# Gate products of two branches in both attention halves and the memory steps, memory gates in five tasks

## The chip, the cores and the metric

The kernel runs on one core of a Trainium2 chip. The number that counts is the device time of one execution in microseconds (us). Five engines with their own instruction streams work on it: PE (matrix products), DVE (vector work), ACT (activations such as exp and sigmoid, and copies), POOL (elementwise work) and SP, which here only issues transfers. Each engine takes its instructions strictly in the order in which they stand in its stream, so an instruction that waits holds up all that stand behind it.

## The reference, cut to what matters

Two layers of a trunk over 256 latent tokens and 256 context tokens, 1024 wide. Each layer is a half feed-forward block, a block of three parallel token mixers, and another half feed-forward block; the change lies in the mixer block alone.

```python
def token_mixers(h, hc, need_ctx, ...):             # h: latent, hc: context, normalised
    qa, ka, va, qb, kb, vb, qm, km, vm, om, gm, gl = split_columns(h @ w_in)
    ...
    y_a = windowed_attention(...)                    # branch 0: 8 heads, window 128, sink logit
    y_b = dense_attention(...)                       # branch 1: 8 heads, all keys
    y_m, y_m_c = mlstm_mixer(...)                    # branch 2: conv + silu, scans, 4 heads ("memory")
    y = merge(y_a, y_b, y_m, gl, w_branch, w_out)

def merge(y_a, y_b, y_m, gate_logits, w_branch, w_out):
    y = jnp.stack([y_a, y_b, y_m], axis=-2)
    z = jnp.einsum('btnw,nwd->btnd', y, w_branch)
    g = jax.nn.sigmoid(gate_logits.reshape(gate_logits.shape[:-1] + (N_BRANCH, D_MODEL)))
    return jnp.sum(g * z, axis=-2) @ w_out
```

`gl` are the gate logits: 3 x 1024 columns of the input product, so per branch eight column blocks of 128. They need only the mixer block's input, which is there from the start, not the branches' results. In layer 1 the context tokens need no output any more (`need_ctx` is false), so all of that runs on 256 tokens in place of 512.

## The kernel before, in words

All products are made in fp32 out of rounded pieces: a weight tile is fetched on SP's queue into one of four buffers called raw, ACT writes its rounded part `hi` (L163), DVE the rest `lo` (L164), and each product is then three matmuls, hi·hi, hi·lo and lo·hi (`mm3`, L194 to L196). `run_tasks` goes through one list of tasks, fetches and converts the weights of the next tasks ahead of their use, and calls each task, which writes its instructions; a tile framework then settles the order on each engine, mostly the order of the calls.

`mixer_tasks` builds the list for one mixer block; `weave(a, b)` spreads list b evenly between the members of a. Its stages, in order, and the names used below:

- The input products (q, k, v and so on). W is the number of tokens that need an output, 512 in layer 0 and 256 in layer 1.
- **Attention**, `attn_steps`: one step per branch, block of 128 queries and pair of heads, 16 steps per branch in layer 0 and 8 in layer 1. The steps of branch 0 are the first half, those of branch 1 the second. A step's call writes the scores of its own pair (PE L1012, L1015), their maximum (DVE L1016), the exponentials (ACT L1030), the reciprocal of the sum (DVE L1039) and the normalisation (POOL L1042); then the transposes of the pair scored two steps earlier (PE L1054) with their hi/lo split (ACT L189, DVE L190); then the product with the values of the pair three steps earlier (PE L1069, L1071). So PE, ACT, DVE and POOL form a chain from one step to the next, which is hidden only if PE has other products to make between.
- In the first half these others are `side`: the preparation of the memory's gates (`mgate_steps`: `logsig`, `rows`, `cols`), products of the memory's values (`vm`), the columns of q of branch 1 (`qcols`), and the gate products of branch 0 that are made ahead (`pre_[0]`: 8 in layer 0, 4 in layer 1). In the second half they are the eight convolution tasks (`conv`: 24 matmuls each, then five taps on ACT L956 and DVE).
- **Memory**: `mlstm_steps`: scores (PE L1212), exponentials of the decays (ACT L1225), their products on DVE (L1229), and a step later the sums (PE L1243). With them are woven the merges of branch 0 (`mrg[0]`) and the gate products of branch 1 that are made ahead (`pre_[1]`: 4 in both layers).
- **Merges and readout**: the output gate `om` with `mlstm_readout` (a chain of small DVE operations that ends in L1279), woven with the first half of branch 1's merges; then three more merges; `put_y2`, which transposes the readout (PE L982); the rest of branch 1; branch 2; and the closing.

A gate product is `gate`, 24 matmuls over W columns. `ahead(j)` makes one early: ACT copies it out (L1311), and two of them go as one pair to DRAM (on ACT's queue, L1313). A merge `mk(j)` makes 12 matmuls of branch weights with the branch's result and multiplies by the sigmoid of the gate. For a stored gate the pair is fetched back through SP's queue and one sigmoid is taken of the whole pair, in place (L1328). Otherwise the gate product is made inside the merge and its sigmoid is L1341. Sigmoid, exp and silu belong to different tables of ACT, and a change from one to the other shows in the trace as an ACT_TABLE_LOAD.

`rows` of the memory's gates puts them on 8 partitions as rows (RW), makes four scans and a fifth (L1142, L1144) and ten further DVE operations (L1146 to L1153) into a second buffer (KR), all in one task.

## Time and profile before

| what | before |
|---|---|
| median of 3 runs | 2273.58 us (2269.32 to 2273.76) |
| the profiled execution | 2271.84 us, span 2270.1 us |
| PE busy | 2195.6 us |
| DVE, ACT, POOL busy | 1545.9, 984.6, 133.0 us |
| layer 0: first attention half, second, memory | 129.90, 95.70, 72.10 us |
| layer 1: first attention half, second, memory | 64.60, 66.60, 52.80 us |

The span runs from the first to the last instruction; 1.7 us of the profiled execution's own time lie around it. The stages of the last two rows are cut where PE goes from one to the next. In the rows further below a stage is one line of five engines; what PE's busy time leaves of its length is time in which PE waited. PEclk is the clock granted to PE, 1.00 being the higher of two levels (2.4 GHz), 0.50 the lower (1.2 GHz).

### The profile page before, as it was taken

To read this page: it belongs to the slowest core of one execution; us is meant where nothing else is said; L and a number is where in the kernel's file an instruction comes from. 1 tells how busy PE (TensorE), PEld (TensorE's weight loads), DVE (VectorE), ACT (ScalarE), POOL (GpSimd) and SP (SyncE) were. 2 spreads that over 40 slices of the span, in tenths; PEclk is the share of its full clock that TensorE was granted. 3 is DMA by queue.
4 is the path that set the end of the run, shared out by engine and by line. 5 is a ranking of instruction groups with operands and counts; after the bars stand their busy time and mean duration, and the time that the engine had idled before them with its cause. 6 is when DMAs were issued, how large, how long until landed. Compare 5 with 4: busy or idle time off the path is not lost.

```text
span 2270.1 us, 30607 instructions
## 1 busy us (share of the span) xinstructions
PE 2195.6 (97%) x11666; PEld 1837.6 (81%) x11666; DVE 1545.9 (68%) x2756; ACT 984.6 (43%) x1569; POOL 133.0 (6%) x100
## 2 busy tenths in 40 slices
PE   6999999998999999999999999999999989998998
PEld 4877777787777888888878788777778878997997
DVE  3987775877678664654444378778849787786556
ACT  3322223554588533542222253222226488655444
POOL 0000000013241000000000000000000142000000
PEclk9999999999999999999999999999999999998999
DMA  7665564422213333434433336665634123565554
GB/s 282 214 196 186 165 199 149 125 81 76 94 38 82 119 119 136 142 115 135 129 114 127 103 107 204 195 195 178 223 116 159 57 89 96 167 228 172 189 186 153
DMA packets 126402, 331.36 MB, mean 146 GB/s; under 512 B 12712, under 2 KB 26088, under 8 KB 125488
## 3 DMA queue, kind: packets, MB, share of 16 engines
q1 hardware_dynamic: 111664, 314.02, 43.0%
q10 hardware_dynamic: 14592, 15.40, 2.2%
q8 instruction: 91, 1.49, 0.3%
q14 instruction: 55, 0.45, 0.1%
HBM read 320.91 MB, written 8.47 MB: 145 GB/s over the span
## 4 chain that ended last, share of the span: by engine, by line
PE 84%; DVE 8%; ACT 3%; DMA 2%; issue 2%; POOL 0%; ACTq 0%; POOLq 0%; SPq 0%; DVEq 0%
PE ps L194 26%; PE ps L195 26%; PE ps L196 26%; PE ps L1243 1%; DVE lo L164 1%; DVE sm L1016 1%; ACT t L1030 1%; PE ps L1212 1%; ACT hi L163 1%; PE ps L366 1%; PE ps L1054 1%; PE ps L468 1%; DVE t L190 0%; DVE slot L959 0%; DMA raw<-in_w_gu_dram 0%
## 5 line engine op out<-in xcount | busy, mean ns | idle before, releaser
L163 ACT ACTIVATE hi<-raw 128x1024 fp32r<-128x1024 f32 (+1 forms) x444 | 457.0, 1032 | 766.8 <-PE ps L195 274.7
L194 PE MATMUL ps<-slot,hi 128*128 128x512 f32 (+1 forms) x2232 | 780.5, 351 | 7.7 <-ACT slot L189 5.3
L195 PE MATMUL ps<-slot,hi 128*128 128x512 f32 (+1 forms) x2232 | 776.9, 349 | 0.9 <-DVE slot L190 0.7
L196 PE MATMUL ps<-slot,lo 128*128 128x512 f32 (+1 forms) x2232 | 776.6, 348 | 0.0
L164 DVE TENSOR_TENSOR lo<-raw,hi 128x1024 fp32r<-128x1024 f32 (+1 forms) x444 | 527.1, 1190 | 245.2 <-ACT hi L163 240.7
L194 PEld LDWEIGHTS ps<-slot,hi 128*128 128x128 f32 x2232 | 421.2, 190 | 77.5 <-ACT slot L189 6.6
L195 PEld LDWEIGHTS ps<-slot,hi 128*128 128x128 f32 x2232 | 422.5, 189 | 57.4 <-DVE slot L190 1.7
L196 PEld LDWEIGHTS ps<-slot,lo 128*128 128x128 f32 x2232 | 421.9, 189 | 57.9
L194 PE MATMUL ps<-hi,slot 128*128 128x512 f32 (+2 forms) x1048 | 400.6, 382 | 1.8 <-ACT slot L189 1.1
L196 PE MATMUL ps<-hi,slot 128*128 128x512 f32 (+2 forms) x1048 | 399.5, 382 | 0.0
L195 PE MATMUL ps<-lo,slot 128*128 128x512 f32 (+2 forms) x1048 | 399.5, 381 | 0.0
L358 DVE SCALAR_TENSOR_TENSOR t<-raw,sc,t 128x1024 f32<-128x1024 f32 x224 | 280.5, 1281 | 128.8 <-DMA raw<-in_w_ada_dram 128.5
L1042 POOL TENSOR_SCALAR t<-t,sm 128x512 f32<-128x512 f32 (+1 forms) x96 | 132.9, 1396 | 1767.1 <-DVE sm L1039 1675.7
L194 PEld LDWEIGHTS ps<-hi,slot 128*128 128x128 f32 x1048 | 197.5, 188 | 46.2 <-issue 5.7
L196 PEld LDWEIGHTS ps<-hi,slot 128*128 128x128 f32 x1048 | 197.0, 188 | 39.3
L195 PEld LDWEIGHTS ps<-lo,slot 128*128 128x128 f32 x1048 | 197.3, 188 | 38.8 <-issue 0.2
L189 ACT ACTIVATE slot<-t 128x512 fp32r<-128x512 f32 (+1 forms) x138 | 80.7, 594 | 185.4 <-DVE t L606 160.2
L606 DVE TENSOR_TENSOR t<-ps,t 128x512 f32<-128x512 f32 (+1 forms) x88 | 54.7, 622 | 89.1 <-PE ps L196 87.8
L190 DVE TENSOR_TENSOR slot<-t,slot 128x512 fp32r<-128x512 f32 (+1 forms) x138 | 87.6, 644 | 4.4 <-ACT slot L189 4.1
L1016 DVE TENSOR_REDUCE sm<-ps 128x1 f32<-128x512 f32 (+1 forms) x96 | 54.4, 593 | 22.2 <-PE ps L1015 21.5
L1054 PE MATMUL ps<-ident,t 128*128 128x128 f32 x320 | 47.7, 282 | 18.6 <-POOL t L1042 8.4
L1054 PEld LDWEIGHTS ps<-ident,t 128*128 128x128 f32 x320 | 37.5, 143 | 28.5 <-POOL t L1042 17.3
(198 smaller groups left out, 1670.6 us busy)
## 6 DMA issues: line engine op xcount, KB each, us to landing
raw<-in_w_gu_dram SPq DMA_DIRECT2D x176, 512.0 KB
raw<-in_w_ada_dram SPq DMA_DIRECT2D x128, 512.0 KB
raw<-in_w_down_dram SPq DMA_DIRECT2D x92, 512.0 KB
raw<-in_w_fm_dram SPq DMA_DIRECT2D x64, 512.0 KB
raw<-in_w_br_dram SPq DMA_DIRECT2D x24, 512.0 KB
raw<-in_w_out_dram SPq DMA_DIRECT2D x24, 512.0 KB
...
```

Source lines behind the costliest of these rows:

```text
L163: self.nc.scalar.activation(out=hi, in_=raw, func=AF.Copy)
L164: self.nc.vector.tensor_tensor(out=lo, in0=raw, in1=hi.bitcast(F32), op=ALU.subtract)
L189: self.nc.scalar.activation(out=hi, in_=src, func=AF.Copy)
L190: self.nc.vector.tensor_tensor(out=lo, in0=src, in1=hi.bitcast(F32), op=ALU.subtract)
L194: mm(out, lh, rh, start=start, stop=False, **kw)
L195: mm(out, lh, rl, start=False, stop=False, **kw)
L196: mm(out, ll, rh, start=False, stop=stop, **kw)
L358: v.scalar_tensor_tensor(out=acc, in0=units[0], scalar=c, in1=acc, op0=ALU.mult, op1=ALU.add)
L606: nc.vector.tensor_tensor(out=hid[:, :W], in0=ps[:, :W], in1=hid[:, :W], op=ALU.mult)
L1016: v.tensor_reduce(out=mx[:, e:e + 1], in_=ps[:, :nkey], axis=AX.X, op=ALU.max)
L1042: nc.gpsimd.tensor_scalar(out=t[:, :nkey], in0=t[:, :nkey], scalar1=r[:, e:e + 1], scalar2=None, op0=ALU.mult)
L1054: nc.tensor.transpose(pt[:, n * P:(n + 1) * P], e[n % 2][:, kb * P:(kb + 1) * P], self.ident)
```

## The change

The list `mixer_tasks` is put together in another way; the products themselves stay the same in number and shape.

- **Layer 0**: branch 0's eight gates stay in the first attention half. All eight of branch 1 are now made early: four woven with the convolutions into the second attention half, four with the memory steps. Before, four were made in the memory steps and four inside the merges.
- **Layer 1**: of branch 0's gates four stay in the first half, and the other four, which were made inside the merges in the memory stage, go with the convolutions into the second half. Branch 1's four stay with the memory steps.
- **Branch 2**: two gates are made before their merges and stay in PSUM until then (`held`): one ahead of the merge that stands before `put_y2`, one after that branch's last merge.
- **Merges**: every merge now takes its own sigmoid of W columns into a buffer of its own, before its matmuls (L1355 of the kernel after); the sigmoid of a whole pair in place is gone.
- **Memory's gates**: `rows` is cut into `rows`, `scans` and `decays`; both sets of rows lie in one buffer, on partitions 0 to 7 and 32 to 39, with a small copy of four columns more; `cols` makes its transposes in two groups with two copies. The tasks are placed one by one between others.
- `stored` is a set that exists only while the program is built.

```diff
-VA, VB = 1, 2
-VL = 1, 1, 2
...
-PRE = 8, 4, 0
-PRE_L = 4, 4, 0
+PRE = 4
+HELD = 2
...
-        np_ = PRE if need_ctx else PRE_L
-        pre_, mrg = zip(*[self.merge_tasks(l, n, ms, R, qs, np_[n]) for n in range(3)])
+
+        pre_, mrg = zip(*[self.merge_tasks(l, n, ms, R, qs, m) for n, m in enumerate((8, 8 if need_ctx else PRE, HELD))])
         att = self.attn_steps(qtb, R)
         gates = self.mgate_steps(R)
         kk_ = self.tok_tasks(l, "kk", 256, 4, range(4), ms, kk)
...
             out += qa + qb[:QB] + [([], lambda _: pre(1))] + vt[:1]
             qb = qb[QB:]
         out += kk_ + [([], spill)] + one(self.k_rows) + vt[1:]
-        nv, va, vb = (0, VA, VB) if need_ctx else VL
-        out += vm_[:nv] + one(self.k_cols) + qcols(0) + qb[:QC]
+        out += vm_[:0 if need_ctx else 1] + one(self.k_cols) + qcols(0) + qb[:QC]
         qb = qb[QC:]
-        side = gates[:1] + qb[:1] + gates[1:2] + qb[1:] + vm_[nv:va] + gates[2:] + vm_[va:vb] + qcols(1) + vm_[vb:]
+        if need_ctx:
+            side = [t for p in zip(gates, qb) for t in p] + gates[3:4] + vm_[:1] + gates[4:] + vm_[1:2] + qcols(1) + vm_[2:]
+            side, with_conv, with_mem = weave(side, pre_[0]), pre_[1][:PRE], pre_[1][PRE:]
+        else:
+            side = [t for p in zip(gates, vm_[1:]) for t in p] + gates[3:4] + qcols(1) + gates[4:]
+            side, with_conv, with_mem = weave(side, pre_[0][:PRE]), pre_[0][PRE:], pre_[1]
         na = 4 * len(qtb)
-        out += weave(att[:na], weave(side, pre_[0])) + weave(att[na:], conv)
+        out += weave(att[:na], side) + weave(att[na:], weave(conv, with_conv))
         out += self.silu_task(R, need_ctx)
         mem = self.mlstm_steps(R, qs)
-        out += mem[:1] + self.split_y(R, 0, W) + weave(weave(mrg[0], pre_[1]), mem[1:])
+        out += mem[:1] + self.split_y(R, 0, W) + weave(weave(with_mem, mrg[0]), mem[1:])
         out += self.split_y(R, 1, W)
-        out += weave(self.tok_tasks(l, "om", 512, 2, qtb, ms, om), mrg[1][:np_[1]])
-        out += mrg[1][np_[1]:np_[1] + 3] + [([], put_y2)] + mrg[1][np_[1] + 3:]
+        out += weave(mrg[1][:PRE], self.tok_tasks(l, "om", 512, 2, qtb, ms, om))
+        out += mrg[1][PRE:6] + pre_[2][:1] + mrg[1][6:7] + [([], put_y2)] + mrg[1][7:] + pre_[2][1:]
         out += mrg[2]
...
         def rows(_):
...
-            RW = self.slot([8, 4, 512])
+            R["RK"] = self.slot([P, SLOT])
+            RW = R["RK"][0:8, :2048].rearrange("p (q t) -> p q t", q=4)
...
-            b_r, m_r = RW[:, 2, :], RW[:, 3, :]
-            i_r, f_r = RW[:, 0, :], RW[:, 1, :]
+
+        def parts():
+            RK = R["RK"]
+            RW = RK[0:8, :2048].rearrange("p (q t) -> p q t", q=4)
+            return RK[32:40, :1792].rearrange("p (q t) -> p q t", q=14), RK[32:40, 1792:1796], [RW[:, q, :] for q in range(4)]
+
+        def scans(_):
+            _, _, (i_r, f_r, b_r, m_r) = parts()
...
-            KR = self.slot([8, 14, P])
+
+        def decays(_):
+            KR, ends, (i_r, f_r, b_r, m_r) = parts()
+            v.tensor_copy(ends, b_r.rearrange("p (b t) -> p b t", b=4)[:, :, P - 1])
...
-        return [([], logsig), ([], rows), ([], cols)]
+        return [([], logsig), ([], rows), ([], scans), ([], decays), ([], cols)]
...
-    def merge_tasks(self, l, n, ms, R, qs, npre):
+    def merge_tasks(self, l, n, ms, R, qs, early):
...
+        def held(j):
+            def fn(units):
+                st[j] = gate(units[0])
             return ([("fm", l, 8 + 8 * n + j)], fn)
 
         def mk(j):
...
                     R.setdefault("uhi", []).append(self.slot([P, 4, W], F32R))
                     R.setdefault("ulo", []).append(self.slot([P, 4, W], F32R))
                 units = list(units)
-                if j >= npre:
+                if j >= early:
                     pg = gate(units.pop(0))
-                elif j % 2 == 0:
-                    st["g"] = units.pop(0).rearrange("p (a b) -> p a b", a=2)
-                    nc.scalar.activation(out=st["g"], in_=st["g"], func=AF.Sigmoid)
+                elif n == 2:
+                    pg = st.pop(j)
+                else:
+                    if j % 2 == 0:
+                        st["g"] = units.pop(0).rearrange("p (a b) -> p a b", a=2)
+                    pg = st["g"][:, j % 2, :]
+                g = self.t512()[:, :W]
+                nc.scalar.activation(out=g, in_=pg, func=AF.Sigmoid)
                 if j % 2 == 0:
                     st["br"] = units.pop(0)
                 bu = st["br"]
...
                 for k in range(4):
                     self.mm3(pz[:, :W], bu[0][:, k, c0:c0 + P], bu[1][:, k, c0:c0 + P], R[f"yh{n}"][:, k, :W],
                              R[f"yl{n}"][:, k, :W], k == 0, k == 3)
-                if j < npre:
-                    g = st["g"][:, j % 2, :]
-                else:
-                    g = self.t512()[:, :W]
-                    nc.scalar.activation(out=g, in_=pg, func=AF.Sigmoid)
                 u = R["u"][j // 4][:, j % 4, :]
                 if n == 0:
                     v.tensor_tensor(out=u, in0=pz[:, :W], in1=g, op=ALU.mult)
...
                     v.tensor_tensor(out=u, in0=u, in1=g, op=ALU.add)
                 if n == 2:
                     self.split(R["uhi"][j // 4][:, j % 4, :], R["ulo"][j // 4][:, j % 4, :], u)
-            keys = [("fm", l, 8 + 8 * n + j)] if j >= npre else [("pre", n, j // 2, W)] if j % 2 == 0 else []
+            if j >= early:
+                keys = [("fm", l, 8 + 8 * n + j)]
+            else:
+                keys = [("pre", n, j // 2, W)] if n < 2 and j % 2 == 0 else []
             if j % 2 == 0:
                 keys.append(("br", l, n, j // 2))
             return (keys, fn)
 
-        return [ahead(j) for j in range(npre)], [mk(j) for j in range(8)]
+        return [(held if n == 2 else ahead)(j) for j in range(early)], [mk(j) for j in range(8)]
 
 
 def weave(a, b, head=0, tail=0):
```

Three places in the order of instructions, with the line numbers of each kernel. PE, layer 0, second attention half, from the last transpose (before L1054, after L1058) of one wide step of branch 1 (4 blocks of keys) on, before:

```order
L1054 MATMUL ps_5532<-ident,t_961_5391 128x128
L1069 MATMUL ps_5496<-t_979_5480,slot_3710 128x256
L1071 MATMUL ps_5496<-t_980_5481,slot_3710 128x256
L1069 MATMUL ps_5496<-t_979_5480,slot_3710 128x256
L1071 MATMUL ps_5496<-t_980_5481,slot_3710 128x256
L1069 MATMUL ps_5496<-t_979_5480,slot_3710 128x256
L1071 MATMUL ps_5496<-t_980_5481,slot_3710 128x256
L1069 MATMUL ps_5496<-t_979_5480,slot_3710 128x256
L1071 MATMUL ps_5496<-t_980_5481,slot_3710 128x256
L1012 MATMUL ps_5552<-slot_3755,slot_4815 128x512
L1015 MATMUL ps_5552<-slot_3755,slot_4815 128x512
L1012 MATMUL ps_5556<-slot_3755,slot_4815 128x512
```

and after:

```order
L1058 MATMUL ps_5567<-ident,t_965_5429 128x128
L193 MATMUL ps_5592<-slot_3114,hi_5379 128x512
L194 MATMUL ps_5592<-slot_3116,hi_5379 128x512
L195 MATMUL ps_5592<-slot_3114,lo_5380 128x512
L1073 MATMUL ps_5531<-t_984_5515,slot_3710 128x256
L193 MATMUL ps_5592<-slot_3114,hi_5379 128x512
L194 MATMUL ps_5592<-slot_3116,hi_5379 128x512
L195 MATMUL ps_5592<-slot_3114,lo_5380 128x512
L193 MATMUL ps_5592<-slot_3114,hi_5379 128x512
L1075 MATMUL ps_5531<-t_985_5516,slot_3710 128x256
L1073 MATMUL ps_5531<-t_984_5515,slot_3710 128x256
L1075 MATMUL ps_5531<-t_985_5516,slot_3710 128x256
```

Before, the products with the values (L1069, L1071) are followed at once by the next step's scores (L1012, L1015); after, a convolution (L193 to L195, 24 matmuls in all) stands among and behind them, as other convolutions or gate products do behind the other steps.

ACT, layer 1, the first exponentials of the memory stage (L1225 before, L1241 after), before:

```order
L163 ACTIVATE hi_16013<-raw_15926 128x1024
L1225 ACT_TABLE_LOAD
L1225 ACTIVATE t_2776_16052<-slot_15962,ZN_14750 128x128 x2
L956 ACTIVATE slot_15715<-ps_15928,convb_13914,convw_13912 128x512
L1225 ACTIVATE t_2776_16052<-t_2776_16052,ZN_14750 128x128
L1225 ACTIVATE t_2776_16052<-slot_15962,ZN_14750 128x128 x3
L1225 ACTIVATE t_2776_16052<-t_2776_16052,ZN_14750 128x128
L1225 ACTIVATE t_2777_16069<-slot_15962,ZN_14750 128x128 x5
L163 ACTIVATE hi_16086<-raw_15978 128x1024
L1225 ACTIVATE t_2788_16133<-slot_15962,ZN_14750 128x128 x2
L1225 ACTIVATE t_2777_16069<-t_2777_16069,ZN_14750 128x128
L163 ACTIVATE hi_16090<-raw_15980 128x1024
```

and after:

```order
L1241 ACT_TABLE_LOAD
L1241 ACTIVATE t_2812_16221<-slot_16128,ZN_15237 128x128
L960 ACTIVATE slot_15815<-ps_16017,convb_13946,convw_13944 128x512
L1082 ACTIVATE t_2784_16055<-ps_16002 64x512
L162 ACTIVATE hi_16173<-raw_16063 128x1024
L1355 ACT_TABLE_LOAD
L1355 ACTIVATE t_2806_16183<-raw_15957 128x256
L1355 ACTIVATE t_2808_16199<-raw_15957 128x256
L1241 ACT_TABLE_LOAD
L1241 ACTIVATE t_2812_16221<-slot_16128,ZN_15237 128x128
L1241 ACTIVATE t_2812_16221<-t_2812_16221,ZN_15237 128x128
L960 ACTIVATE slot_15815<-ps_16065,convb_13946,convw_13944 128x512
```

Before, one table load stands ahead of a run of exponentials; after, a merge's sigmoids (L1355) stand among them, with a load ahead of and behind them. In the whole of layer 1's memory stage and merges the stream has 10 loads before and 14 after, in layer 0's 10 and 20; in the attention halves it has 9 and 9 before, 6 (layer 0) and 5 (layer 1) after.

DVE, layer 0, first attention half, the scans of the memory's gates (L1142, L1144 before; L1153, L1155 after), before:

```order
L1016 TENSOR_REDUCE sm_4112<-ps_4113 128x1
L1142 SCALAR_TENSOR_TENSOR slot_4072<-ones,slot_4072 8x128 x4
L1144 SCALAR_TENSOR_TENSOR slot_4072<-slot_4072 8x512
L1151 TENSOR_TENSOR slot_4098<-slot_4072 8x128
L1146 TENSOR_TENSOR slot_4098<-slot_4072 8x512
L1153 TENSOR_SCALAR slot_4098<-slot_4098,slot_4072 8x128
L1151 TENSOR_TENSOR slot_4098<-slot_4072 8x128
L1153 TENSOR_SCALAR slot_4098<-slot_4098,slot_4072 8x128 x2
L1151 TENSOR_TENSOR slot_4098<-slot_4072 8x128
L1153 TENSOR_SCALAR slot_4098<-slot_4098,slot_4072 8x128 x3
L1151 TENSOR_TENSOR slot_4098<-slot_4072 8x128
L1016 TENSOR_REDUCE sm_4112<-ps_4118 128x1
```

and after:

```order
L1153 SCALAR_TENSOR_TENSOR slot_4072<-ones,slot_4072 8x128
L1023 SCALAR_TENSOR_TENSOR sm_4123<-sm_4125,nsink_3233 128x2
L189 TENSOR_TENSOR t_692_4150<-ps_4151,t_691_4149 128x512
L1039 TENSOR_TENSOR sm_4141<-sinkr_3235,sm_4123 128x2
L1153 SCALAR_TENSOR_TENSOR slot_4072<-ones,slot_4072 8x128 x3
L1155 SCALAR_TENSOR_TENSOR slot_4072<-slot_4072 8x512
L1041 TENSOR_TENSOR sm_4124<-sm_4124,sm_4141 128x2
L1159 COPY slot_4072<-slot_4072 8x4
L1160 TENSOR_TENSOR slot_4072<-slot_4072 8x512
L1043 RECIPROCAL sm_4145<-sm_4124 128x2
L189 TENSOR_TENSOR t_692_4150<-ps_4158,t_691_4149 128x512
L1085 TENSOR_TENSOR slot_4173<-ps_4063,t_696_4174 64x2x128 x2
```

Before, the scans and the decays are one unbroken run between two maxima; after, they are cut by the attention's own operations (L1023, L189, L1039, L1041, L1043).

## Rows read from the trace of the kernel before

**Rows 1.** The page's first part: busy time, share of the span, instructions.

```profile
PE 2195.6 (97%) x11666; PEld 1837.6 (81%) x11666; DVE 1545.9 (68%) x2756; ACT 984.6 (43%) x1569; POOL 133.0 (6%) x100
```

**Rows 2.** Windows, by stage: length; PE, PEld, DVE, ACT, POOL busy; PEclk; DMA share; GB/s.

```profile
483.30:613.20 129.90, 124.07 (x673) 102.39 (x673) 92.39 (x247) 67.66 (x154) 41.83 (x32) 1.00 0.22 73
613.20:708.90 95.70, 85.28 (x470) 71.25 (x469) 71.00 (x147) 75.00 (x133) 39.96 (x32) 0.98 0.26 75
708.90:781.00 72.10, 72.10 (x397) 62.59 (x396) 56.61 (x233) 52.14 (x107) 0.00 (x0) 1.00 0.25 81
...
1783.00:1847.60 64.60, 57.66 (x374) 48.47 (x373) 51.58 (x130) 34.37 (x77) 25.32 (x16) 0.97 0.16 52
1847.60:1914.20 66.60, 59.96 (x369) 51.98 (x368) 50.94 (x101) 53.91 (x88) 25.74 (x16) 0.97 0.28 86
1914.20:1967.00 52.80, 52.80 (x431) 51.93 (x430) 43.48 (x146) 46.56 (x89) 0.00 (x0) 1.00 0.41 136
```

**Rows 3.** Waits of PE, layer 0's first half: waiter, releaser, us, times, longest.

```profile
PE ps L1054 <- DVE t L190: 3.2, 1, 3.2
PE ps L1069 <- ACT t L1030: 2.0, 1, 2.0
```

**Rows 4.** Timeline of DVE there: start, us, line, operation, count.

```profile
514.66 1.35 DVE L1142 TENSOR_TENSOR_SCAN slot<-ones,slot 8x128 f32<-8x128 f32 x4
```

**Rows 5.** Waits of PE, layer 0's second half.

```profile
PE ps L1054 <- POOL t L1042: 6.0, 8, 1.2
```

**Rows 6.** Timeline of PE there; in brackets the idle time before, and its releaser.

```profile
634.98 1.06 PE L1054 MATMUL ps<-ident,t 128*128 128x128 f32 x8 [1.03 <-DVE t L190]
649.23 0.33 PE L1054 MATMUL ps<-ident,t 128*128 128x128 f32 x1 [0.42 <-POOL t L1042]
650.77 0.98 PE L1054 MATMUL ps<-ident,t 128*128 128x128 f32 x7 [1.21 <-POOL t L1042]
653.42 0.50 PE L194 MATMUL ps<-slot,hi 128*128 128x512 f32 x1 [0.73 <-ACT t L1030]
663.02 1.06 PE L1054 MATMUL ps<-ident,t 128*128 128x128 f32 x8 [1.05 <-ACT t L1030]
```

**Rows 7.** Windows: the lower clock, then steady products of 512 and of 256 columns.

```profile
622.05:625.46 3.41, 3.41 (x14) 3.03 (x13) 1.54 (x4) 2.88 (x7) 0.00 (x0) 0.50 0.00 1
...
880.00:900.00 20.00, 20.00 (x88) 16.22 (x88) 8.87 (x10) 7.04 (x10) 0.00 (x0) 1.00 0.52 184
2012.00:2032.00 20.00, 20.00 (x174) 20.00 (x173) 14.41 (x23) 10.69 (x17) 0.00 (x0) 1.00 0.68 236
```

**Rows 8.** Waits of PE, layer 1's first half.

```profile
PE ps L1069 <- DVE t L190: 2.2, 2, 1.7
```

**Rows 9.** Waits of PE, layer 1's second half.

```profile
PE ps L1054 <- POOL t L1042: 2.4, 3, 1.2
```

**Rows 10.** Timeline of ACT, layer 1's memory stage.

```profile
1935.18 1.28 ACT L1341 ACT_TABLE_LOAD   x1
1936.47 0.39 ACT L1341 ACTIVATE t<-ps 128x256 f32<-128x256 f32 x1
...
1954.90 0.40 ACT L1225 ACTIVATE t<-t,ZN 128x128 f32<-128x128 f32 x1
```

**Rows 11.** Timeline of PE, the end of that stage.

```profile
1964.26 2.28 PE L1243 MATMUL ps<-slot,t 128*128 128x129 f32 x19
```

**Rows 12.** Groups of ACT, whole program: busy, mean ns, idle before.

```profile
L1328 ACT ACT_TABLE_LOAD x9 | 11.5, 1283 | 7.7 <-DMA raw<-pre 7.5
```

**Rows 13.** Timeline of PE, layer 0: last product of om, then put_y2.

```profile
811.72 0.40 PE L196 MATMUL ps<-hi,slot 128*128 128x512 f32 x1
...
839.84 1.36 PE L982 MATMUL ps<-ident,t 128*128 128x128 f32 x11
```

**Rows 14.** Timeline of DVE, layer 0: the readout's last operation.

```profile
828.04 1.14 DVE L1279 SCALAR_TENSOR_TENSOR t<-slot,sm,t 128x128 f32<-128x128 f32 x4
```

**Rows 15.** Waits of PE, layer 1, memory to put_y2.

```profile
PE ps L982 <- DVE t L1279: 0.5, 1, 0.5
```

21 lines of the change are left out of this document (13 added, 8 removed).

## The prediction

> **What bounds the kernel now.** I read the busy times first: PE works 2195.6 us of a span of 2270.1 us [rows 1], so some 74.5 us of waiting are all that a new order can win, as the change leaves PE's products alike. The windows by stage say where they lie [rows 2]: the attention halves of layer 0 leave 129.90 - 124.07 = 5.83 and 95.70 - 85.28 = 10.42 us, those of layer 1 6.94 and 6.64, the two memory stages nothing. That is 29.8 us; the change touches nearly nothing of the rest. No other engine is full in those halves (ACT at most 81%, DVE 80%), so PE waits for the chain of a step, not for an engine's total. The waits name POOL's normalisation and the split behind the transposes [rows 3, 5, 8, 9], and the timeline shows the pattern [rows 6]: in layer 0's second half two wide steps in a row with no product between lose about 1.0 us (1.03 and 1.05), three lose 2.36 (0.42 + 1.21 + 0.73). The three such runs of three steps in that half add up to 8.0 of its 10.4 us. A second loss hangs on the first: after waits PE ran 3.41 us at 0.50 of its clock, the lower level [rows 7], and the mean clock of the second half in layer 0 and of both in layer 1 is 0.97 to 0.98 [rows 2].
>
> **The price of a gate product.** 88 matmuls of 512 columns take 20 us and 174 of 256 columns take 20 us [rows 7], so 24 of them are 5.5 us in layer 0 and 2.8 in layer 1. Moving one costs nothing by itself: what it adds to one stage it takes from another.
>
> **Layer 0, first half.** It keeps its eight gates. New is that scans and decays are cut up between the attention's DVE work. Before, they are one run that begins at 514.66 [rows 4], the split stands behind it, and PE waits 3.2 us for that split [rows 3]. I take this one wait away: -3.2 us. Bounds: -5.0, if the wait of 2.0 on an exponential goes too, and -1.0, if pieces of the run still stand before a split.
>
> **Layer 0, second half.** Twelve products stand between its steps in place of eight, and by the new order no run of three steps without one is left, only five runs of two: three wide, two narrow. Wide ones lose 1.0 us [rows 6]; the narrow ones are in what is left of before, 10.4 - 8.0 - 2.1 = 0.3 us for all of them. 3 x 1.0 + 0.3 = 3.3 us in place of 10.4: -7.1. Bounds: -9.4 (0.2 each), and -4.0, if ACT, with four more conversions and copies, lengthens the chain. The stretch at half clock follows the first waits of this half, before its first convolution; that convolution now stands earlier. 3.41 us at half clock hold 1.7 us of work: I take -1.5 (0 to -1.7).
>
> **Layer 0, memory and merges.** The same four gates are made there, so PE's cover stays. ACT works 52.1 of 72.1 us [rows 2] and gets ten table loads more, by the order, of 1283 ns [rows 12]: 12.8 us, still below 72. PE is never late there now, with eight loads in that stretch. I take +0.5; bounds 0 and +4 (three of the ten loads in full). The two more pairs that are stored and fetched, 512 KB each, go in under a DMA share of 0.25 [rows 2]: nothing. They are issued on ACT's queue and SP's, and a fetch can make only a sigmoid wait; today the sigmoids of nine fetched pairs wait 7.5 us for theirs, 0.8 each [rows 12], inside that cover.
>
> **Layer 0, put_y2.** Four merges of branch 1 lose their gates, 5.5 us each, and they are what hides the readout. om's last product starts at 811.72 and put_y2 at 839.84 [rows 13]; the readout's last operation ends at 828.04 + 1.14 = 829.2 [rows 14], 17 us after om. Left as cover are three merges of 12 matmuls (2.8 each) and the held gate (5.5): 13.9 us, and put_y2's first blocks are ready earlier, which hides 1.4 more. So PE waits 17 - 15.3, about +1.5 us, bounds 0 and +3. Late next is the split behind put_y2, with a merge and the second held gate (8.3 us) over it: nothing.
>
> **Layer 1, first half.** Four gates as before; the value products are spread further and the scans are cut up as in layer 0. Its waits are short and hang on splits that come late [rows 8]. I take -2.5 of the 6.94 (-4 to 0), and -0.7 of the 1.9 us that a mean clock of 0.97 over 64.6 us stands for (0 to -1.7).
>
> **Layer 1, second half.** Twelve products in place of eight: one between any two steps, and no pair of steps without one. Layer 1's two halves also had nine table loads and now have five, because the sigmoids of stored pairs no longer fall into them. But waits are there already beside single convolutions, on POOL [rows 9], so not all goes: -4.5 of 6.64 (-2 to -6), and of the clock -1.2 (0 to -1.7).
>
> **Layer 1, memory.** Here the change takes something away: four gates, 4 x 2.76 = 11.0 us of PE work, go to the half before. ACT works 46.6 of 52.8 us [rows 2]. Its last exponential ends at 1954.90 + 0.40 = 1955.3 [rows 10] and PE needs it at 1964.26 [rows 11]: 9.0 us to spare. After, PE is there 11.0 us earlier; ACT gets four loads more (5.1), four conversions less (-4.2) and a few sigmoids (+0.9), so it is 1.8 us later. 11.0 + 1.8 - 9.0 = +3.8 us. Bounds: +1, if the loads that left the half before let ACT start ahead, and +7, if the added loads fall in front of awaited exponentials. put_y2 waits 0.5 us now [rows 15] and gets a longer cover through the held gate: -0.5 (0).
>
> **Weighed against the Trainium skill.** In the trace a load takes 1.28 us, and the activation behind it starts 0.01 us after its end (1935.18 + 1.28, then 1936.47) [rows 10]. The Trainium skill, ScalarE: Activation LUTs, "What ACT_TABLE_LOAD costs", gives 1283 ns for the load and some 1380 ns of drain for every switch, 2.66 us in all, which speaks against a sigmoid per merge between exponentials. By it layer 1's memory would cost 4 x 1.38 = 5.5 us more than my term. The load agrees with the trace, the drain isn't to be seen in it.
>
> **The sum.** -3.2 - 7.1 - 1.5 + 0.5 + 1.5 - 2.5 - 0.7 - 4.5 - 1.2 + 3.8 - 0.5 = -15.4 us on the profiled execution's 2271.84: 2256.4. That execution lies 1.7 us below the median of the runs, 2273.58, so the median to expect is **2258 us**. All terms at their good ends give -29, 2245; all at their bad ends +7, 2281.
>
> **The rivals.** What a measurement can tell from no change here is some 0.2%, 4.5 us: faster is below 2269.0, slower above 2278.1.
>
> (a) Half the gain. The halves may be bound by ACT and DVE in single steps rather than by a lack of products: for it speaks that layer 1's second half waits beside convolutions too, against it the pattern of runs of two and three steps [rows 6]. Half of the attention's terms (20.7) is 10.3; with the costs of 5.3: -5.0, 2268.5.
>
> (b) Slower: ScalarE sets the end of the memory stages. Each sigmoid now stands between exponentials and takes two loads along, and behind it in ACT's order are the exponentials that the sums (L1243) need. If all fourteen added loads were exposed (18.0), with about seven sigmoids (4.2), four more fetched pairs awaited at 0.8 each (3.3), and the 2.0 us by which layer 1 loses more cover than ACT has to spare (11.0 - 9.0), it would be 27.5 us against the attention's 20.7, with the readout's 1.0 about +8: 2281. It decides where ACT's last exponential comes later than PE: layer 0 has 20 us of room in the stage, layer 1 9 us. For it speaks ACT's 88% in layer 1, against it that layer 0 has room. With the drain that the Trainium skill gives (ScalarE: Activation LUTs, the section named above), 14 x 1.38 = 19.3 us would come on top, 2300; since the trace shows none, that has 0.02 of this rival's chance.
>
> (c) The gates don't end up between the steps, since the framework orders by its own rules: 2273.6, no change. The order of the changed kernel shows them there, so this is left with little.
>
> **How the numbers follow.** The forecast gets 0.60, (a) 0.22, (b) 0.14, (c) 0.04. The forecast's own range is 2248 to 2269, and nearly all of it is faster; of (a) a good half is. Faster 0.58 + 0.13 = 0.71; slower is (b), 0.13, with a hundredth of it ending within the bound; the rest, 0.16, is no change. For 8 times in 10 the range takes in the forecast and (a), 2248 to 2274, and leaves out most of (b).
>
> **What would show it.** Right: layer 0's second half about 14 us longer (22 us of gates less 8), with 3 us of waits and a clock of 1.00; the wait of 3.2 us on L190 gone; memory stage of layer 0 with PE full; layer 1's with 3 to 4 us of waits on exponentials; put_y2 in layer 0 waiting 0 to 3 us on the readout. Wrong: waits of PE in the second halves that stay at 10 and 6 us beside the gates; long waits of L1243's sums for exponentials with a table load right before them; a stretch at half clock behind such a wait.

## The result

The changed kernel takes 2247.82 us (median of 4 runs, 2245.66 to 2250.63) beside 2273.15 of the kernel before (4 runs, 2269.32 to 2273.76): a ratio of 0.9893, interval 0.9875 to 0.9911, or some 25 us less. That is faster, as forecast, and 10 us below the forecast of 2258, on the lower edge of the forecast's range (2248, missed by 0.2). The profiled execution took 2245.83 us, 26.0 less than that of before.

The page's first part for the kernel after, to be held beside [rows 1]:

```profile
PE 2186.8 (97%) x11666; PEld 1833.2 (82%) x11666; DVE 1546.0 (69%) x2760; ACT 997.9 (44%) x1594; POOL 135.4 (6%) x100
```

PE does the same 11666 products. The span shrank by 26.0 us, PE's busy time by 8.8 of them: so only 17 us are waits that went, and 9 us are the same products taking less time. Part of that is the clock, part is something the prediction did not have (the last of the experiments).

Windows of the kernel after, columns as in [rows 2]: layer 0's two attention halves, layer 1's two halves and its memory stage. For layer 1 the cuts lie at the first product of each stage; [rows 2] cut its first half 1.7 us earlier and 3.6 us later, so the same two cuts of before stand beneath in a fence of their own.

```profile
481.70:611.80 130.10, 124.93 (x673) 103.33 (x673) 93.20 (x248) 67.85 (x154) 40.37 (x32) 0.99 0.22 74
611.80:718.90 107.10, 104.24 (x565) 87.72 (x565) 78.22 (x155) 79.62 (x146) 41.10 (x32) 1.00 0.26 84
1772.10:1831.40 59.30, 54.48 (x353) 47.07 (x354) 49.87 (x126) 30.79 (x71) 27.13 (x16) 0.94 0.17 59
1831.40:1902.70 71.30, 70.89 (x483) 64.51 (x482) 59.49 (x113) 60.93 (x106) 26.57 (x16) 1.00 0.38 112
1902.70:1945.50 42.80, 42.80 (x345) 41.96 (x344) 32.90 (x131) 41.79 (x81) 0.00 (x0) 1.00 0.39 128
```

```profile
1784.70:1844.00 59.30, 53.04 (x346) 44.79 (x347) 46.66 (x123) 30.86 (x71) 22.21 (x15) 0.97 0.15 50
1844.00:1914.30 70.30, 63.66 (x394) 55.21 (x394) 54.33 (x104) 56.49 (x93) 28.86 (x18) 0.98 0.28 87
```

What PE's busy time leaves of the length is the wait. In layer 0's second half it fell from 10.42 to 2.86 us, in layer 1's from 6.64 to 0.41, and the clock there is 1.00 in both. In the first halves it is 5.17 after 5.83, and 4.82 after 6.26, with a lower clock than before. Whether a stage gained is read by its length less the gates moved in: 24 products of 512 columns are 5.5 us, of 256 columns 2.76. Each length is that of one profiled execution. Layer 0's first half took 129.3 to 131.1 us in this kernel and in four of the experiments that have the same order there, so a net of 1 us is neither a gain nor a loss.

| stretch, from PE's first product in it | before | after | gates moved | net | forecast |
|---|---|---|---|---|---|
| up to layer 0's first half | 483.4 | 481.7 | | -1.7 | 0 |
| layer 0, first half | 129.9 | 130.1 | | +0.2 | -3.2 |
| layer 0, second half | 95.6 | 107.1 | +21.8 | -10.4 | -8.6 |
| layer 0, memory and merges | 207.7 | 187.0 | -21.8 | +1.1 | +2.0 |
| between the two mixers | 868.1 | 866.2 | | -1.9 | 0 |
| layer 1, first half | 59.2 | 59.4 | | +0.1 | -3.2 |
| layer 1, second half | 70.3 | 71.3 | +11.0 | -10.1 | -5.7 |
| layer 1, memory and merges | 122.4 | 111.3 | -11.0 | -0.1 | +3.3 |
| tail (last network and output) | 233.4 | 230.1 | | -3.3 | 0 |
| sum | 2270.1 | 2244.0 | | -26.1 | -15.4 |

### The profile page after: what moved, and what is told of

Read it like the earlier page. It is cut to its first block, busy times and chain, and to the rows that moved or that the text cites. A ratio compares the mean times of both kernels' runs of the same rounds, so it can differ in the third digit from the quotient of the medians.

```text
span 2244.0 us, 30646 instructions
## 1 busy us (share of the span) xinstructions
PE 2186.8 (97%) x11666; PEld 1833.2 (82%) x11666; DVE 1546.0 (69%) x2760; ACT 997.9 (44%) x1594; POOL 135.4 (6%) x100
## 4 chain that ended last, share of the span: by engine, by line
PE 89%; DVE 6%; ACT 2%; issue 1%; DMA 1%; ACTq 0%; DVEq 0%
PE ps L193 27%; PE ps L194 27%; PE ps L195 27%; PE ps L1259 1%; PE ps L1058 1%; PE ps L1228 1%; PE ps L366 1%; DVE lo L163 1%; PE ps L1073 1%; PE ps L468 1%; PE ps L1075 1%; PE ps L1016 1%; DVE sm L1020 1%; DMA slot<-in_w_ada_dram 1%; PE ps L1019 1%
## 5 line engine op out<-in xcount | busy, mean ns | idle before, releaser
L193 PE MATMUL ps<-slot,hi 128*128 128x512 f32 (+1 forms) x2232 | 778.4, 351 | 6.0 <-ACT slot L188 4.9
L195 PE MATMUL ps<-slot,lo 128*128 128x512 f32 (+1 forms) x2232 | 773.6, 347 | 0.0
L193 PEld LDWEIGHTS ps<-slot,hi 128*128 128x128 f32 x2232 | 420.5, 189 | 75.9 <-ACT slot L188 6.2
L195 PEld LDWEIGHTS ps<-slot,lo 128*128 128x128 f32 x2232 | 421.5, 189 | 57.4
L193 PE MATMUL ps<-hi,slot 128*128 128x512 f32 (+2 forms) x1048 | 400.3, 382 | 1.9 <-ACT slot L188 1.1
L195 PE MATMUL ps<-hi,slot 128*128 128x512 f32 (+2 forms) x1048 | 398.8, 381 | 0.0
L358 DVE SCALAR_TENSOR_TENSOR t<-raw,sc,t 128x1024 f32<-128x1024 f32 x224 | 280.3, 1281 | 129.9 <-DMA raw<-in_w_ada_dram 129.7
L193 PEld LDWEIGHTS ps<-hi,slot 128*128 128x128 f32 x1048 | 197.1, 188 | 46.2 <-issue 6.6
L195 PEld LDWEIGHTS ps<-hi,slot 128*128 128x128 f32 x1048 | 196.7, 188 | 39.8
L188 ACT ACTIVATE slot<-t 128x512 fp32r<-128x512 f32 (+1 forms) x138 | 80.5, 594 | 172.3 <-DVE t L606 153.5
L189 DVE TENSOR_TENSOR slot<-t,slot 128x512 fp32r<-128x512 f32 (+1 forms) x138 | 87.6, 643 | 5.1 <-ACT slot L188 4.6
L603 ACT ACTIVATE t<-ps 128x512 f32<-128x512 f32 (+1 forms) x88 | 46.4, 527 | 24.2 <-DVE t L426 16.5
L189 DVE TENSOR_TENSOR t<-ps,t 128x512 fp32r<-128x512 f32 x80 | 54.2, 684 | 1.9 <-ACT t L188 1.7
```

Source lines behind the costliest of these rows:

```text
L188: self.nc.scalar.activation(out=hi, in_=src, func=AF.Copy)
L189: self.nc.vector.tensor_tensor(out=lo, in0=src, in1=hi.bitcast(F32), op=ALU.subtract)
L193: mm(out, lh, rh, start=start, stop=False, **kw)
L195: mm(out, ll, rh, start=False, stop=stop, **kw)
L358: v.scalar_tensor_tensor(out=acc, in0=units[0], scalar=c, in1=acc, op0=ALU.mult, op1=ALU.add)
L603: nc.scalar.activation(out=hs["sg"][:, :W], in_=ps[:, :W], func=AF.Silu)
```

## The experiments

Each kernel was timed beside the kernel before on the same chip; the ratio is to that, with its interval. Each expectation names its own theories; where the prediction's terms are one of them, it says so (B in l0_gates, l1_gates, spread and after_oldgates). A difference between two kernels counts in their times where the intervals are apart; otherwise it is read from stages and waits.

**The parts of the change, one at a time.** Three kernels hold one part each: the gates of layer 0 with the two held ones (l0_gates), the gates of layer 1 alone (l1_gates), the five tasks of the memory's gates alone (spread). A part that is off has the old order; in all three the sigmoid of a stored pair is made in place, as before. The memory's gates keep their new form in all three (one buffer, the small copy, two groups of transposes): in l0_gates and l1_gates `rows`, `scans` and `decays` of that form run as one.

```diff
-HELD = 2
+GATES = (1, 0)     # l1_gates (0, 1); spread (0, 0)
+SPREAD = (0, 0)    # spread (1, 1)
+HELD = (2, 0)      # l1_gates and spread (0, 0)
...
+            run = [([], lambda _: [gates[n][1](_) for n in (1, 2, 3)])]
+            nv, va, vb = (0, 1, 2) if need_ctx else (1, 1, 2)
+            side = gates[:1] + qb[:1] + run + qb[1:] + vm_[nv:va] + gates[4:] + vm_[va:vb] + qcols(1) + vm_[vb:]
```

> Layer 0's part of the change alone: four gates of branch 1 with the convolutions, four with the memory steps, the two held gates of layer 0; memory gates as one run, one sigmoid for a stored pair, layer 1 as before. Theory A (the second halves' fillers bring nearly all, as the two traces put side by side say): layer 0's mixer falls from 433.3 us to 424 (-9), layer 1's stays at 252, time 2264. Theory B (the terms of the prediction for these places, -7.1 - 1.5 + 0.5 + 1.5): -6.6, time 2266.5. Theory C (a good part of the 25 us came through parts of the program that the change does not touch, which are 7 us shorter in the profile after): untouched parts shorter here too by some 3 us, time about 2261.

l0_gates took 2268.07 us, 0.9977 (0.9968 to 0.9986). The second half gained 10.6 us net, but memory and merges lost 6.9. PE's timeline at put_y2 (L1003 there) shows more than half of the loss in one wait on the readout's last operation:

```profile
847.01 0.47 PE L1003 MATMUL ps<-ident,t 128*128 128x128 f32 x1 [3.91 <-DVE t L1312]
```

No theory had that: the gain stands, but the price at put_y2 is larger than the prediction's 1.5 us, and in the full change it is nearly absent. What differs in the merges of layer 0 is the sigmoid (in place per pair here, per merge there); after_pair, below, takes that up.

> Layer 1's part alone: branch 0's gates e to h go from the memory stage to the second attention half; no held gates, memory gates as one run, one sigmoid for a stored pair, layer 0 as before. Theory A: layer 1's mixer from 251.9 to 242 us (-10), time 2263. Theory B (the prediction's terms, -4.5 - 1.2 + 3.8): -1.9, time 2271. Theory C: as A or B and the untouched parts shorter by some 3 us.

l1_gates took 2267.22 us, 0.9974 (0.9964 to 0.9984). Its second half lost all its waiting, 10.0 us net, and memory and merges did not pay (-0.9; without the added loads the prediction's working would still give 11.0 - 9.0 = +2.0):

```profile
1848.40:1919.70 71.30, 71.30 (x490) 65.18 (x490) 60.59 (x114) 61.16 (x109) 32.07 (x18) 1.00 0.36 116
```

PE is busy for the whole of the window. Gates between the steps are enough for it, without the five tasks. The kernel as a whole gained less than that, 6.5 us, since stretches without this change came out longer in its profile: layer 0's halves 131.8 and 97.1 us for 129.9 and 95.6, layer 1's first half 61.4 for 59.2. In layer 0's first half, here and in l0_gates, the new form of the memory's gates as one run has a wait of 4.1 us on the split in place of the 3.2 of [rows 3]; much of the rest goes with a lower clock (0.96 in layer 0's second half here, 0.94 in layer 1's first).

> The five tasks of the memory gates alone, placed one by one in both layers' first halves as in the kernel after; all gates of the merges as before. Theory A (the wait behind the run of DVE work only moves to the next late operation): first halves 129.9 and 59.2 us keep their lengths within 1 us, time 2273. Theory B (the prediction's terms -3.2, -2.5 and -0.7): 2267, no wait of 3 us on the split in layer 0's first half.

spread took 2271.11 us, 0.9992 (0.9983 to 1.0002): no difference. Its waits in layer 0's first half (waiter, releaser, us, times, longest):

```profile
PE ps L1075 <- DVE t L191: 2.7, 2, 2.0
PE ps L1090 <- ACT t L1051: 2.2, 1, 2.2
```

The wait of 3.2 us of [rows 3] is gone, and 2.7 us in two pieces have come in its place; the second row is the wait of 2.0 us that stood in [rows 3] too. So the five tasks move the wait and don't remove it.

**The two held gates.** after_noheld sets HELD to 0, and both gates are made inside their merges.

```diff
-HELD = 2
+HELD = 0
```

> The kernel after without the two held gates: branch 2's first two gates are made inside their merges again. Theory A (they are the cover of the readout in layer 0): the transposes of put_y2 come 5.7 us earlier and wait for the readout's third and fourth block, some 5.5 us in layer 0 and nothing in layer 1, time 2253. Rival (the readout is covered anyway): 2248, no wait over 1 us at put_y2.

2252.80 us, 0.9911 (0.9896 to 0.9926): 5.0 slower than the change by the medians. In its profile layer 0's memory and merges lost 6.0. PE waits 4.1 us at put_y2, in place of 0.2, and the clock of the 10 us behind is 0.80:

```profile
PE ps L986 <- DVE t L1295: 4.1, 2, 2.9
```

So the held gate covers put_y2 in layer 0, as the prediction had it.

**One sigmoid for a pair.** after_pair has all of the change but the sigmoid per merge: a stored pair's is made in place, once, which leaves 38 table loads by the order in place of 50.

```diff
-                    pg = st["g"][:, j % 2, :]
-                g = self.t512()[:, :W]
-                nc.scalar.activation(out=g, in_=pg, func=AF.Sigmoid)
+                        nc.scalar.activation(out=st["g"], in_=st["g"], func=AF.Sigmoid)
+                    g = st["g"][:, j % 2, :]
...
```

> The kernel after with the sigmoid as before: one for a stored pair, in place, as soon as the pair is there; 38 table loads by the order in place of 50. Theory A (layer 0's part alone left a wait of 3.9 us at put_y2 that the kernel after does not have, and the difference between them is this sigmoid: it stands early in ACT's order, waits for the fetched pair, and holds up the readout's work behind it): layer 0 from the memory stage to the closing 187.0 to 192 us, time about 2253. Theory B (table loads cost time, as the Trainium skill's advice to group by table says, or the rival of the prediction): faster than the kernel after, 2243 to 2246. Theory C: the loads and the place of the sigmoid are all covered, 2248.

2253.32 us, 0.9911 (0.9896 to 0.9926). With twelve loads fewer it is 5.5 us slower by the medians; in its profile 4.8 us lie in layer 0's memory and merges, and 1.7 in layer 1's first half, with the same waits and a clock of 0.92 for 0.94. Rival (b) of the prediction falls with that, and with the change itself: from the memory stage to the closing PE waits 0.5 us in layer 0 and 0.2 in layer 1, all of it on DVE. By the Trainium skill, ScalarE: Activation LUTs, "What ACT_TABLE_LOAD costs", twelve switches more would take ScalarE 12 times 2.66, some 32 us, an estimate from that page; the trace has its 1283 ns for each load, and no run here shows the rest. The 4.8 us come from DVE. Its timeline at the readout, first of after_pair, then of the change:

```profile
828.73 0.68 DVE L1370 TENSOR_TENSOR raw<-ps,raw 128x512 f32<-128x512 f32 x1
...
831.63 0.69 DVE L1371 TENSOR_TENSOR slot<-slot,raw 128x512 f32<-128x512 f32 x1
...
834.03 1.14 DVE L1295 SCALAR_TENSOR_TENSOR t<-slot,sm,t 128x128 f32<-128x128 f32 x4
...
844.05 1.14 DVE L1295 SCALAR_TENSOR_TENSOR t<-slot,sm,t 128x128 f32<-128x128 f32 x4
```

```profile
834.89 1.14 DVE L1295 SCALAR_TENSOR_TENSOR t<-slot,sm,t 128x128 f32<-128x128 f32 x4
...
839.89 1.14 DVE L1295 SCALAR_TENSOR_TENSOR t<-slot,sm,t 128x128 f32<-128x128 f32 x4
840.94 1.28 DVE L1368 TENSOR_TENSOR t<-ps,t 128x512 f32<-128x512 f32 x2
842.14 1.29 DVE L1369 TENSOR_TENSOR slot<-slot,t 128x512 f32<-128x512 f32 x2
```

L1295 ends each block of the readout. With the pair's sigmoid the merges' multiplications and additions (L1370, L1371) stand between these blocks in DVE's order, and the last block comes at 844.05; with the sigmoid per merge they stand behind it (L1368, L1369), and it comes at 839.89, when PE is just arriving. PE waits 3.9 us in the one and 0.2 in the other:

```profile
PE ps L986 <- DVE t L1295: 3.9, 1, 3.9
```

**The old order of the memory's gates.** after_oldgates puts `rows` back together in its old place and shape, and leaves the rest of the change.

```diff
+         nv, va, vb = (0, 1, 2) if need_ctx else (1, 1, 2)
+         side = gates[:1] + qb[:1] + gates[1:2] + qb[1:] + vm_[nv:va] + gates[2:] + vm_[va:vb] + qcols(1) + vm_[vb:]
...
-        return [([], logsig), ([], rows), ([], scans), ([], decays), ([], cols)]
+        return [([], logsig), ([], rows), ([], cols)]
```

> The kernel after with the memory's gates as before: three tasks, two buffers, and the other tasks of the first halves placed as before. Theory A (in the first halves one wait only took the place of another): first halves 130 and 59 us as in both kernels, time 2248. Theory B (the terms of the prediction for them, -3.2 and -3.2): 2254, with the wait of 3 us on the split back.

2251.34 us, 0.9902 (0.9887 to 0.9917), 3.5 slower than the change by the medians, with intervals that overlap. But the first halves account for little: 131.5 for 130.1, and 59.2 for 59.4. The tail, in which the two kernels don't differ in their code, accounts for 3.8, and the stretch between the mixers for 1.3. The first halves' waits are there again as in [rows 3]:

```profile
PE ps L1058 <- DVE t L189: 3.1, 1, 3.1
PE ps L1073 <- ACT t L1034: 2.0, 1, 2.0
```

**More products in the first halves.** If those waits are a lack of products, gates between the steps must remove them. better1 makes two more gates in each first half (and passes others on: layer 0 stores two of branch 2, layer 1 two more of branch 1). Its edit also spreads the other tasks of the first halves between the gates, where the change spreads the gates between those tasks, so it moves DVE's pieces too.

```diff
-            side, with_conv, with_mem = weave(side, pre_[0]), pre_[1][:PRE], pre_[1][PRE:]
+            side, with_conv, with_mem = weave(pre_[0] + pre_[1][:2], side), pre_[1][2:6], pre_[1][6:] + pre_[2][:2]
...
-            side, with_conv, with_mem = weave(side, pre_[0][:PRE]), pre_[0][PRE:], pre_[1]
+            side, with_conv, with_mem = weave(pre_[0][:6], side), pre_[0][6:] + pre_[1][:2], pre_[1][2:]
```

> The kernel after with two more gate products in each first half: layer 0 makes branch 1's gates a and b there, c to f with the convolutions, g, h and two stored ones of branch 2 with the memory steps, and holds the next two; layer 1 makes six gates of branch 0 there, the last two and branch 1's a and b with the convolutions, c to f with the memory steps. The memory stages keep four gates each. If the first halves' waits (5.2 and 4.8 us, with 1 and 3 us lost to the lower clock) come from a lack of products between the steps, as in the second halves: half of it goes, -7, 2241. If they come from the order of DVE's work, which the products do not change: 2248, the same waits on L163's and the split's places.

2238.78 us, 0.9848 (0.9831 to 0.9864), 9 below the change. Its first halves:

```profile
483.00:618.60 135.60, 134.97 (x722) 110.77 (x722) 93.30 (x245) 70.20 (x155) 40.21 (x30) 1.00 0.25 84
...
1767.20:1827.30 60.10, 56.52 (x401) 49.95 (x402) 51.89 (x127) 34.28 (x76) 24.83 (x15) 1.00 0.27 93
```

Layer 0's has 0.6 us of waiting left and takes 5.4 us more for 10.9 us of added products: -5.5. So products between the steps, as they stand here, remove its waits; what more of them do and what their new places do was not parted. Layer 1's takes 0.8 more for 5.5: -4.7, of which 1.2 are waits (3.6 left after 4.8) and most of the rest is the clock, 1.00 for 0.94 of 59.3 us (3.6).

**The decays later.** better2 is better1 with `decays` and `cols` moved into the second halves, out of the first halves' chains.

```diff
-            side = [t for p in zip(gates, qb) for t in p] + gates[3:4] + vm_[:1] + gates[4:] + vm_[1:2] + qcols(1) + vm_[2:]
+            side = [t for p in zip(gates, qb) for t in p] + vm_[:2] + qcols(1) + vm_[2:]
...
+        late = gates[3:] + [([], lambda _: None)]
```

> As the one before, and the decays and columns of the memory's gates go from the first to the second attention half. If the waits of the first halves come from the order of DVE's work, that run of DVE operations now has more products around it: 2 to 4 us less than the one before, at most 1 us of it given back in the second half. If they come from a lack of products, no change against it.

2258.81 us, 0.9936 (0.9921 to 0.9951), 20 above better1: 7.7 in layer 0's mixer, 9.7 in layer 1's, 3.8 in the tail (on which more below). Neither forecast came. The first halves gained nothing by it: 136.8 for 135.6, with 3.2 us of waits for 0.6 in layer 0, and 59.6 for 60.1. Layer 0's is one row of its waits: the product that makes the memory's columns (L1184) needs the copies behind their transposes (L1182), and with the decays late these are late. Layer 1's 9.7 are in several smaller waits and a lower clock, 0.96 in its second half.

```profile
PE ps L1184 <- DVE Z L1182: 7.6, 1, 7.6
```

**Layer 1's put_y2, and the cover of its memory stage.** better1 left a wait of 2.8 us at layer 1's put_y2. better3 puts both held gates of layer 1 ahead of it. no_cover is better1 with the four gates of layer 1's memory stage made in the merges instead, which takes the cover by gates away there.

```diff
-        out += mrg[1][PRE:6] + h[:1] + mrg[1][6:7] + [([], put_y2)] + mrg[1][7:] + h[1:]
+        e = 1 if need_ctx else 2
+        out += mrg[1][PRE:6] + h[:e] + mrg[1][6:7] + [([], put_y2)] + mrg[1][7:] + h[e:]
```

```diff
-        pre_, mrg = ... enumerate((8, 8 if need_ctx else 6, 2 if need_ctx else 0))
+        pre_, mrg = ... enumerate((8, 8 if need_ctx else 2, 2 if need_ctx else 0))
```

> The kernel better1 (two more gates in each first half) with both held gates of layer 1 ahead of put_y2. Better1 waits 2.8 us there for the readout, and a gate product of 256 columns covers 2.8: 2236, the wait gone. If the wait only moves behind put_y2 (the split of its transposes is then late for branch 2): 2239.

> The kernel better1 with no gate products in layer 1's memory stage: branch 1's c to f are made inside their merges, after the stage. PE then reaches the last sums 11.4 us earlier, ACT, with four conversions and four copies less, is done 5.7 us earlier; better1 has 2.0 us between ACT's last exponential and the sums. Theory A (ACT sets the end of the stage where the cover goes): some 3.7 us of waits on exponentials there, in one or several places; the wait of 2.8 us at put_y2 goes, since its cover grows; 2240. Theory B (ACT has room, its work can start as much earlier): no waits in the stage, 2236.

better3 took 2236.90 us, 0.9841 (0.9826 to 0.9855): the lowest median of all, 10.9 below the change, 1.9 below better1, whose interval overlaps. The wait fell from 2.8 to 1.0, and 0.8 of it came back at the split behind put_y2, so 1.0 us is left as its gain. Layer 1's mixer doesn't show even that: it took 240.4 us for 239.3, as its second half ran at 0.98 of the clock; the 1.9 us lie in layer 0's memory and merges (174.5 for 176.4), where the two kernels don't differ. no_cover took 2239.18 us, 0.9849 (0.9833 to 0.9865). Its waits from the memory stage on, which better1 has not:

```profile
PE ps L193 <- ACT slot L188: 1.2, 1, 1.2
...
PE ps L194 <- DVE slot L189: 0.8, 1, 0.8
```

They are 2.0 us, on the split of branch 1's result (`split_y`, L188 and L189), which stands in ACT's order behind the last exponential and a sigmoid with its load:

```profile
1925.48 0.39 ACT L1243 ACTIVATE t<-t,ZN 128x128 f32<-128x128 f32 x1
1925.89 1.28 ACT L1357 ACT_TABLE_LOAD   x1
1927.18 0.42 ACT L1357 ACTIVATE t<-raw 128x256 f32<-128x256 f32 x1
1927.50 1.13 ACT L188 ACTIVATE slot<-slot 128x512 fp32r<-128x512 f32 x2
```

So here ACT does set the end of the stage, as theory A had it, at a smaller price. Its mixer of layer 1 is even 0.5 us shorter than better1's, since put_y2 no longer waits; its tail is 4.1 longer. With eleven more microseconds of cover gone, layer 1's memory stage loses about 2 us.

**The stretches that the change doesn't touch.** In the kernels so far the tail takes 229.6 to 231.4 us in some and 233.4 to 234.3 in the others, at equal code; the stretch between the mixers takes from 864.9 to 868.1. Nothing in the tail's waits differs. What differs is where the pool puts the last network's four operand buffers (upper and lower parts, two each) among its 13 places of 8256 bytes. Counted from the pool's start, they lie at places 12, 8, 2 and 0 in the change and at 12, 7, 6 and 2 in the kernel before; of thirteen kernels, the eight with all four at even places have the short tail, the five with an odd one the long one. after_swap exchanges the buffers of upper and lower parts among the same four places. after_odd takes two unused buffers ahead of them, so that they lie at 2, 0, 6 and 11; each gets a one-column clear on POOL.

```diff
+            if l == 1 and k == 2:
+                nc.gpsimd.memset(self.slot([P, 16])[:, 0:1], 0.0)
+                nc.gpsimd.memset(self.slot([P, 16])[:, 0:1], 0.0)
```

> The kernel after, the same instructions in the same order, with the buffers of the rounded part and the rest of every normalised input exchanged. The parts of the program that the change does not touch were shorter in some of the kernels (the stretch between the mixers 866 or 868 us, the tail behind the last mixer 230 or 234 us), by a product of 24 matmuls that takes 2.77 or 2.83 us with the same instructions. Theory A (where the operands lie decides that): other lengths of these stretches, by 1 us or more in one of them, 2248 to 2254. Theory B (something else does): 866 and 230 us as in the kernel after, 2248.

> The kernel after with two more buffers of the same pool taken (one column each set by POOL) just before the last feed-forward block takes the four buffers of its normalised input, so that these lie elsewhere; PE, ACT and DVE have the same instructions in the same order. In the twelve kernels profiled so far the tail behind the last mixer took 230 to 231 us where all four lay an even number of buffers (8256 bytes each) from the pool's start, and 233 to 234 us where one lay an odd number, with one kernel between. Here they are the second, the start itself, the sixth and the eleventh. Theory A (the place decides): the tail goes from 230.1 to some 233.5 us, its products from 2.77 to 2.83 us, time 2251. Theory B (something else that goes along with it): 230, 2248.

after_swap took 2247.13 us, 0.9884 (0.9870 to 0.9899), with 230.1 us in its tail: which part lies where does not matter. after_odd took 2251.50 us, 0.9903 (0.9887 to 0.9920), 3.7 above the change by the medians, with 232.1 us in its tail. The same 240 products of the last network by line (busy us, mean ns, idle before), of the kernel before, of the change and of after_odd:

```profile
L194 PE MATMUL ps<-slot,hi 128*128 128x256 f32 x240 | 67.4, 285 | 0.0
```

```profile
L193 PE MATMUL ps<-slot,hi 128*128 128x256 f32 x240 | 66.6, 281 | 0.0
```

```profile
L193 PE MATMUL ps<-slot,hi 128*128 128x256 f32 x240 | 67.0, 283 | 0.0
```

The number of products is the same and these wait for nothing, yet each takes longer when the operand buffers have moved: the place of buffers changes the pace. From one start to the next, 24 of them take 2.83 us in the kernel before, 2.77 in the change and 2.82 in after_odd. By its tail after_odd is between the two groups, though, and l0_gates, all at even places (12, 8, 2, 6), ran at the slow pace in the later part of its tail. So odd and even is no full rule, and why the place matters stays open.

## Why the prediction was right, and where it was off

**The mechanism held.** PE waited in the second halves because steps followed each other with no product between. With gates between most of them, layer 0's keeps 2.86 us of waits (3.3 forecast), in three pieces near the 1.0 us that the runs of two had let expect:

```profile
PE ps L1058 <- ACT t L1034: 1.0, 1, 1.0
PE ps L1075 <- DVE t L189: 0.9, 1, 0.9
PE ps L193 <- ACT t L1034: 0.7, 1, 0.7
```

With the clock back at 1.00 that gave 10.4 us where 8.6 were forecast. l0_gates and l1_gates show that the gates alone do it (10.6 and 10.0 us).

**Layer 1, second half: a term mis-sized.** Forecast -4.5 and -1.2, measured -10.1. The step that failed is "waits are there already beside single convolutions, on POOL [rows 9], so not all goes": all but 0.4 us went, so 6.2 in place of 4.5; one more product of 2.76 us between two steps covers those gaps too. The clock (0.98 to 1.00 of 70.3 us) gave the 1.4 us about as forecast. That makes 7.6; of the other 2.5, eight products with the values (L1073, L1075) that now stand in the first half are about 1 us, and the rest was not taken apart.

**Both first halves: wrong.** -3.2 and -3.2 were forecast, nothing came. The step that failed is "I take this one wait away": for layer 0 it read the run of scans on DVE [rows 4] as the cause of the wait of 3.2 us, which did go, but it took nothing else on DVE to be late in its place. The other wait of [rows 3] stayed, before and after:

```profile
531.74 0.39 PE L1069 MATMUL ps<-t,slot 128*128 128x256 f32 x1 [1.99 <-ACT t L1030]
```

```profile
526.49 0.39 PE L1073 MATMUL ps<-t,slot 128*128 128x256 f32 x1 [2.18 <-ACT t L1034]
...
544.65 0.55 PE L1058 MATMUL ps<-ident,t 128*128 128x128 f32 x3 [1.98 <-DVE t L189]
```

The wait of 1.98 us is new, with one of 0.50 between the two. Ahead of its split DVE has another unbroken run, the preparation of branch 1's q (L741 to L762, 6.2 us):

```profile
536.59 0.69 DVE L762 TENSOR_REDUCE qss<-t 128x8 f32<-128x512 f32 x1
...
542.12 0.68 DVE L762 TENSOR_REDUCE qss<-t 128x8 f32<-128x512 f32 x1
542.72 1.28 DVE L1020 TENSOR_REDUCE sm<-ps 128x1 f32<-128x512 f32 x2
543.91 0.68 DVE L189 TENSOR_TENSOR t<-ps,t 128x512 fp32r<-128x512 f32 x1
```

The prediction's own bound for it (-1.0, "if pieces of the run still stand before a split") was the nearer end in size, though what stood before the split was another run. A further loss follows the wait of 2.18 us: 3.4 us at the lower level of the clock.

```profile
526.90:530.30 3.40, 3.40 (x15) 2.92 (x15) 1.75 (x5) 2.21 (x6) 2.44 (x2) 0.53 0.77 287
```

In layer 1 the waits did fall, by 1.4 us, but the clock's 0.94 in place of 0.97 took 1.8 back. spread and after_oldgates agree: over both halves the five tasks are 1.2 us shorter than the old run in one pair of kernels (the change and after_oldgates) and 0.6 longer in the other (spread and the kernel before), which is within the scatter. The gates of better1 gain 5.5 and 4.7 there.

**Layer 0, memory and put_y2: right in size (+1.1 for +2.0), by another balance.** PE waits 0.2 us at put_y2 in place of 1.5. The prediction held the sigmoid per merge to be a cost; it is what keeps the merges' work behind the readout on DVE. That the size came out right is in part luck. Without it the term would have been +5.9 by after_pair's stage, and without the held gates +7.1 by after_noheld's.

**Layer 1, memory: +3.8 forecast, nothing came.** The step that failed is "11.0 + 1.8 - 9.0": it sets a PE that is 11.0 us earlier against an ACT that starts its exponentials with the stage, as before; an earlier start stood only as the good bound (+1). The timeline of ACT, the first exponential before the change, then the first and last after it, and of PE where it needs the last:

```profile
1912.80 0.69 ACT L1225 ACTIVATE t<-slot,ZN 128x128 f32<-128x128 f32 x2
```

```profile
1893.38 0.40 ACT L1241 ACTIVATE t<-slot,ZN 128x128 f32<-128x128 f32 x1
...
1939.49 0.39 ACT L1241 ACTIVATE t<-t,ZN 128x128 f32<-128x128 f32 x1
```

```profile
1941.61 3.29 PE L1259 MATMUL ps<-slot,t 128*128 128x129 f32 x28
```

The first comes 9.3 us ahead of PE's first product of the stage (1902.7), where it led by 1.5 us before: 7.8 us more, since the half before hands its results over earlier (argued, not tested by itself). From first to last the exponentials take 46.5 us in place of 42.5, with the added loads among them. So the 9.0 us to spare become 9.0 + 7.8 - 4.0 - 11.1, and ACT ends 1.7 us before PE. no_cover shows that the mechanism is real where more cover goes: 2.0 us.

**What the sum left out.** The parts that the change touches came to -19.2 us for -15.4. The other 6.9 us lie in stretches it doesn't touch: 5.2 in the slower pace before (between the mixers 1.9, tail 3.3), which after_odd ties in the tail to the place of buffers and which for the stretch between the mixers is only argued; and 1.7 before the first mixer, where the experiments' lengths scatter from 481.7 to 483.1. That the total came within 11 us of the forecast is in part luck, since errors cancelled: the first halves stayed 6.7 us short of their terms, while the second halves brought 6.2, memory and merges 4.3 and the untouched stretches 6.9 more.

**The rivals.** (a), half the gain, falls with the second halves. (b), ScalarE as the bound, falls with after_pair, and with layer 1's 1.7 us to spare; in no_cover, with 11 us less cover, it shows with 2.0 us. (c) was excluded by the order, and by the waits.
